# Attention of a four-layer decoder: fp32r halves replaced by fp32 operands

## The chip, the cores and the metric

One NeuronCore of a Trainium2 chip runs the whole program in one launch. The metric is the device time of an execution in microseconds (us); lower is better.

## What is computed

The reference is a decoder trunk of four layers over 256 positions and 1024 channels, all fp32. A layer is a token mixer, an output projection, a LayerNorm, a SwiGLU feed-forward of width 2816 and another LayerNorm. The mixer has 12 heads of width 64 and, beside them, 4 heads that attend to 256 memory tokens. Its kind is `i % 3`: 0 (layers 0 and 3) is attention over the keys that an indexer selects, 1 (layer 1) is dilated attention in three head groups that are merged by their softmax denominators (its values are 192 wide, four of them), 2 (layer 2) is plain causal attention at this length.

```python
for i in range(DEPTH):                       # DEPTH = 4
    kind, j = i % N_MIXERS, i // N_MIXERS
    if kind == 0:   mix = dsa_attention(q, k, v, qi, wi, ki)
    elif kind == 1: mix = dilated_attention(q, k, v)
    else:           mix = moba_attention(q, k, v)
    mo = memory_attention(qm, mk, mv)
    mixed = concat([mix, mo], -1) @ w_out[i]
    x = layer_norm(ALPHA * x + mixed, ln1_g[i], ln1_b[i])
    x = layer_norm(ALPHA * x + swiglu(x, w_gate_up[i], w_down[i]), ln2_g[i], ln2_b[i])
# attention of a head: softmax(q k^T / 8, masked) v
```

## The kernel before

All weights come once from HBM as 400 pieces of 128 x up to 1024 (`load`, line 206, on SyncE's queue, four `raw` buffers). Each piece is split in two fp32r parts: ScalarE casts the high part (`emit_hi`, L214), VectorE or GpSimd subtracts it to get the low part (`emit_lo`, L230 and L228). The activations `x` are held as two parts too. A product is then three fp32r matmuls in a row, high by high, and the two mixed ones (`mm3`, L256 to L258); a fourth, low by low, is left out.

```python
256  mm(out, lhsT=ah, rhs=bh, start=first, stop=False)
257  mm(out, lhsT=ah, rhs=bl, start=False, stop=False)
258  mm(out, lhsT=al, rhs=bh, start=False, stop=last)
```

The order on TensorE (PE) is that of the program. The main line issues the projections and the feed-forward, some 12 matmuls at a time, and after each such step `tick` advances a list of tasks, Python generators. One `yield n` of a task waits for n ticks, so that PE has other work while ScalarE (ACT) and VectorE (DVE) do the task's part. The constants `W_ROT`, `W_K`, `W_EXP`, `W_NORM`, `W_PT` are these waits. `join` ticks without issuing main work when something is needed at once. The other engines are ordered by the scheduler. Eight PSUM banks of 128 x 512 go round through all tasks (`tk(self.banks)`).

A mixer works by pairs of heads (128 columns) and by two blocks `tb` of 128 positions; block 0 sees 128 keys, block 1 sees 256. A pair's task runs so:

- `rotated` (L473): rotary positions, then two PE transposes of the fp32 rows, which put q and k with channels on partitions.
- `qk_task`: q and k are split in fp32r parts. The two parts of a head's 64 channels are laid on the two halves of the 128 partitions (`q_parts`, L267 and L272; `k_parts`, L265 and L270), and k is also copied crosswise on ACT (`k_cross`, L492 and L493). One matmul over all 128 partitions then does two products of halves at once.
- `logits` (L500 for 128 keys, L504 for 256): one or two fp32r matmuls of 256 columns a head, both heads in one bank.
- `exps` and `softmax`: mask and row minimum (L526 and, for 128 keys, L524), exponentials back into the bank (L529), then reciprocal and division of the whole matrix (L541, L542).
- `turned` (L555): PE transposes of the fp32 probabilities, one of 128 x 128 for each head and key block; the result is split in `pa`/`pb` high and low (L265, L270).
- `attend` (line 563): `mm3` of a 128-column pair of values against both heads' probabilities (256 columns), of which the two diagonal quarters are kept (`diag_out`: four instructions, L265 and L270, of 64 partitions).

The memory heads (`mem_task`) and the dilated layer (`dil_task`, `dil_combine`) use the same helpers. The indexer (`select_task`) uses `logits` with `kb` shared by its eight heads.

Of the kernel before, what the change touches and what calls it, by code (L numbers as in the profile page):

```python
# [112 lines left out]
class K:  # L113
    def __init__(self, tc, io, ctx):
# [22 lines left out]
        self.kks = one([128, 2, 2, S], "k", NKB, F32R)  # L137
        self.sts = one([128, 64], "st", 12)
        self.xT = (T([128, 8, S], F32R, "xh"), T([128, 8, S], F32R, "xl"))
        self.memT = (T([128, 8, S], F32R, "mh"), T([128, 8, S], F32R, "ml"))  # L140
        self.mk = [T([128, 2, 2, S], F32R, f"mk{i}") for i in range(2)]
        self.mv = (T([128, 2, 256], F32R, "mvh"), T([128, 2, 256], F32R, "mvl"))
# [336 lines left out]
    def q_parts(self, dst, src, scale=None):  # L479

        lo, hi = slice(0, 64), slice(64, 128)
        return [(dst[lo, 0], dst[hi, 0], src[lo], scale), (dst[hi, 1], dst[lo, 1], src[hi], scale)]

    def k_parts(self, dst, src):

        d = dst.rearrange("p h a t -> p a h t")
        n = src.shape[1]
        return d[:, 0], d[:, 1], src[:, None, :].to_broadcast([128, 2, n]), None

    def k_cross(self, dst):  # L490
        lo, hi = slice(0, 64), slice(64, 128)
        self.nc.scalar.copy(dst[hi, 0], dst[lo, 0])  # L492
        self.nc.scalar.copy(dst[lo, 1], dst[hi, 1])  # L493

    def logits(self, b, q, ks, nk):

        mm = self.nc.tensor.matmul
        for h in range(2):
            if nk == 128:
                mm(b[:, h * 256:h * 256 + 256].rearrange("p (a s) -> p a s", a=2), lhsT=q[:, h], rhs=ks[h][:, :, 0:128],  # L500
                   start=True, stop=True)
            else:
                for part in range(2):
                    mm(b[:, h * 256:h * 256 + 256], lhsT=q[:, h], rhs=ks[h][:, part], start=part == 0, stop=part == 1)  # L504

    def pair_logits(self, b, q, kb, nk):
        self.logits(b, q, [kb[:, h] for h in range(2)], nk)

    def read_logits(self, b, nk):
        if nk == 128:  # L510
            L = b.rearrange("p (h a s) -> p h a s", h=2, a=2)
            return L[:, :, 0], L[:, :, 1]
        return (b.rearrange("p (h s) -> p h s", h=2),)

    def exps(self, L, e, mn, sm, mask=None, dst=None):


        nc = self.nc
        dst = L[0] if dst is None else dst
        if mask is None:  # L520
            nc.vector.tensor_reduce(mn, L[0], op=OP.min, axis=AX.X)
        else:
            if len(L) == 2:
                nc.vector.tensor_tensor(e, L[1], mask[:, None, :].to_broadcast([128, 2, 128]), op=OP.add)  # L524
            for h in range(2):
                nc.vector.tensor_tensor_reduce(out=L[0][:, h], in0=L[0][:, h], in1=mask if len(L) == 1 else e[:, h], op0=OP.add,  # L526
                                               op1=OP.min, scale=1.0, scalar=3e38, accum_out=mn[:, h:h + 1])
        for h in range(2):
            nc.scalar.activation(dst[:, h], L[0][:, h], AF.Exp, bias=mn[:, h:h + 1], scale=-1.0, accum_out=sm[:, h:h + 1])  # L529

    def softmax(self, nk, product, mask=None):

        nc = self.nc
        b = yield from self.tk(self.banks)
        st = yield from self.tk(self.sts)
        e = yield from self.tk(self.es[nk])
        product(b)
        L = self.read_logits(b, nk)
        self.exps(L, e, st[:, 0:2], st[:, 2:4], mask)
        yield W_EXP  # L540
        nc.vector.reciprocal(st[:, 4:6], st[:, 2:4])  # L541
        nc.vector.tensor_tensor(e, L[0], st[:, 4:6, None].to_broadcast([128, 2, nk]), op=OP.mult)  # L542
        self.banks.put(b)
        self.sts.put(st)
        yield W_NORM
        return e

    def turned(self, e, nk):
# [7 lines left out]
        self.split((pT[0], pT[1], p, None))  # L556
# [5 lines left out]
    def attend(self, e, nk, vs, vi, col, mix, kb, tb):  # L562
        pT = yield from self.turned(e, nk)
        nsb = nk // 128
        while vs[vi] is None or not vs[vi][2]:
            yield 1
        v = vs[vi][0]
        b = yield from self.tk(self.banks)
        o = b[:, 0:256].rearrange("p (h t) -> p h t", h=2)
        for sb in range(nsb):  # L570
            self.mm3(o, (v[0][:, sb, col:col + 128], v[1][:, sb, col:col + 128]),
                     (pT[0][:, sb], pT[1][:, sb]), sb == 0, sb == nsb - 1)
        self.pTs[nsb].put(pT)
        self.diag_out(mix[kb], tb, o)
        self.banks.put(b)

    def diag_out(self, dst, tb, o):
        ts = slice(tb * 128, tb * 128 + 128)
        rs = [slice(h * 64, h * 64 + 64) for h in range(2)]
        self.split(*((dst[0][r, ts], dst[1][r, ts], o[r, h], None) for h, r in enumerate(rs)))  # L580

    def qk_task(self, bank, tb, kb, q, flags):
        b, p = yield from self.rotated(bank, tb)
        q[tb] = yield from self.tk(self.qs)
        k = kb[:, :, :, tb * 128:tb * 128 + 128]
        self.split(self.k_parts(k, p[:, 1]), *self.q_parts(q[tb], p[:, 0], SCALE))
        self.k_cross(k)
        self.banks.put(b)
        yield W_K
        flags.add(("k", tb))  # L590

    def head_task(self, bank, tb, kb, q, flags, masks, vs, vi, col, mix, kbi):
# [5 lines left out]
        def product(b):  # L598
            self.pair_logits(b, q[tb], kb, nk)
# [4 lines left out]
        e = yield from self.softmax(nk, product, masks[tb])  # L604
        yield from self.attend(e, nk, vs, vi, col, mix, kbi, tb)
# [7 lines left out]
    def v_piece(self, l, i, tbs, vrec):  # L613
        v = vrec[0]
        for tb in tbs:
            b = self.a_mode(self.xT, tb, ("v", l, i), tb == 1)
            self.split((v[0][:, tb], v[1][:, tb], b[:, 0:256], None))
# [7 lines left out]
    def mk_piece(self, l):  # L625
        b, p = self.t_mode(self.memT, ("mk", l, 0))
        self.split(*(self.k_parts(self.mk[pp], p[:, pp]) for pp in range(2)))
        for pp in range(2):
            self.k_cross(self.mk[pp])
# [3 lines left out]
    def mv_piece(self, l):  # L633
        for sb in range(2):
            b = self.a_mode(self.memT, sb, ("mv", l, 0), sb == 1)
            self.split((self.mv[0][:, sb], self.mv[1][:, sb], b[:, 0:256], None))
# [3 lines left out]
    def qm_piece(self, l):  # L640
        b, p = self.t_mode(self.xT, ("qm", l, 0))
        qm = [self.take(self.qms, "qm") for _ in range(2)]
        self.split(*(x for pp in range(2) for x in self.q_parts(qm[pp], p[:, pp], SCALE)))
# [4 lines left out]
    def mem_task(self, qm, pp, tb, mix):  # L648
        ts = slice(tb * 128, tb * 128 + 128)

        def product(b):
            self.pair_logits(b, qm[pp][:, :, ts], self.mk[pp], S)
        e = yield from self.softmax(S, product)
        yield from self.attend(e, S, [[self.mv, 0, True]], 0, pp * 128, mix, 6 + pp, tb)

    def mem_tasks(self, qm, mix):
        def run(pp):
# [3 lines left out]
            self.qms.put(qm[pp])  # L661
# [3 lines left out]
    def ki_task(self, bank, tb, kb, wi, kg, kbb, flags):  # L665
# [21 lines left out]
        self.split((kb[:, 0, 0, tb * 128:tb * 128 + 128], kb[:, 0, 1, tb * 128:tb * 128 + 128], b[:, 0:128], None))  # L687
# [513 lines left out]
```

## Time and profile before

| | |
|---|---|
| median of 3 runs | 1353.04 us (1347.6 to 1353.33) |
| the profiled execution | 1351.82 us, of which the span from the first to the last instruction is 1350.0 us |
| TensorE | 1287.3 us busy, 9186 matmuls, mean granted clock 0.983 |
| VectorE | 897.5 us busy, 1940 instructions |
| ScalarE | 762.9 us busy, 1512 instructions |
| GpSimd | 316.4 us busy, 277 instructions |
| DMA | 225.65 MB, 167 GB/s |

The terms below are made against the profiled execution: 1351.82 us, 1.82 us more than its span and 1.22 us under the median. A row of a group of instructions gives the line, the engine, the operation, what it writes and reads, its shape and count; then the busy time and the mean of one in ns; then the idle time of the engine just before, and who ended it. Matmuls overlap, so that their mean is longer than the step from one to the next; the step is read from the order of time. Layer 0's mixer runs from 0 to about 150 us, layer 1's from 375 to 490, layer 2's from 700 to 805, layer 3's from 1015 to 1140; the rest is output projection and feed-forward.

### The profile page before, as it was taken

What the parts mean: (1) busy time and instruction counts of PE and PEld (TensorE: products, weight loads), DVE (VectorE), ACT (ScalarE), POOL (GpSimd) and SP (SyncE); (2) the same over time, 40 slices, a digit from 0 to 9 for tenths busy, and PEclk for the clock granted to TensorE, in tenths of its full rate; (3) what the DMA queues carried; (4) which work ended last, traced back from release to release, by engine and by line L of the source; (5) the groups of instructions that cost most, each with busy time, mean ns of one, the idle gap of its engine ahead of it and who ended that gap; (6) DMA issues with size and microseconds to landing.
All of it is one profiled execution on the core that took longest, in us unless ns stands there. A gap on an engine that the chain in (4) does not pass through costs nothing. (4 is left out here: it accounts for less than half of the span.)

```text
span 1350.0 us, 24249 instructions
## 1 busy us (share of the span) xinstructions
PE 1287.3 (95%) x9186; PEld 1212.5 (90%) x9186; DVE 897.5 (66%) x1940; ACT 762.9 (57%) x1512; POOL 316.4 (23%) x277
## 2 busy tenths in 40 slices
PE   6889899999999789999999999999999899999997
PEld 5879799999999779999989989999999898899996
DVE  7887775555578886555567877555568997655555
ACT  5668754444469745444447986444445897544441
POOL 3434440000045343000034444000014533300000
PEclk9989999999999889999999999999999999999999
DMA  8443356556564136565545345666546333655551
GB/s 300 126 149 110 110 180 199 187 188 184 170 203 150 70 103 240 185 189 180 183 155 180 133 141 169 206 185 188 186 138 218 127 125 126 203 188 188 187 176 59
DMA packets 63190, 225.65 MB, mean 167 GB/s; under 512 B 7776, under 2 KB 7776, under 8 KB 63072
## 3 DMA queue, kind: packets, MB, share of 16 engines
q1 hardware_dynamic: 62784, 224.10, 50.2%
q8 instruction: 72, 1.18, 0.4%
q14 instruction: 46, 0.38, 0.1%
q10 hardware_dynamic: 288, 0.00, 0.0%
HBM read 223.02 MB, written 1.05 MB: 166 GB/s over the span
## 5 line engine op out<-in xcount | busy, mean ns | idle before, releaser
L214 ACT CAST wh<-raw 128x1024 fp32r<-128x1024 f32 (+1 forms) x402 | 420.8, 1048 | 318.6 <-PE bank L257 177.2
L230 DVE TENSOR_TENSOR wl<-raw,wh 128x1024 fp32r<-128x1024 f32 (+1 forms) x294 | 378.2, 1288 | 273.9 <-ACT wh L214 269.1
L228 POOL TENSOR_TENSOR wl<-raw,wh 128x512 fp32r<-128x512 f32 x216 | 296.7, 1399 | 727.7 <-ACT wh L214 718.2
L256 PE MATMUL bank<-xh,wh 128*128 128x256 f32 x1344 | 382.1, 284 | 0.0
L257 PE MATMUL bank<-xl,wh 128*128 128x256 f32 x1344 | 381.2, 284 | 0.0
L258 PE MATMUL bank<-xh,wl 128*128 128x256 f32 x1344 | 381.2, 284 | 0.0
L257 PEld LDWEIGHTS bank<-xl,wh 128*128 128x128 f32 x1344 | 258.6, 192 | 1.2
L256 PEld LDWEIGHTS bank<-xh,wh 128*128 128x128 f32 x1344 | 258.6, 192 | 1.3
L258 PEld LDWEIGHTS bank<-xh,wl 128*128 128x128 f32 x1344 | 258.5, 192 | 0.0
L256 PE MATMUL bank<-wh,xh 128*128 128x256 f32 (+1 forms) x768 | 228.5, 298 | 2.8 <-ACT wh L214 1.9
L257 PE MATMUL bank<-wl,xh 128*128 128x256 f32 (+1 forms) x768 | 221.6, 289 | 2.5 <-DVE wl L230 2.3
L258 PE MATMUL bank<-wh,xl 128*128 128x256 f32 (+1 forms) x768 | 221.7, 289 | 0.8 <-DVE xl L270 0.6
L256 PE MATMUL bank<-wh,fth 128*128 128x512 f32 x480 | 189.8, 395 | 0.4 <-ACT fth L265 0.4
L257 PE MATMUL bank<-wl,fth 128*128 128x512 f32 x480 | 188.2, 392 | 0.0
L258 PE MATMUL bank<-wh,ftl 128*128 128x512 f32 x480 | 188.0, 392 | 0.0
L256 PEld LDWEIGHTS bank<-wh,xh 128*128 128x128 f32 x768 | 150.1, 196 | 4.0 <-ACT wh L214 2.4
L257 PEld LDWEIGHTS bank<-wl,xh 128*128 128x128 f32 x768 | 150.1, 195 | 3.1 <-DVE wl L230 3.1
L258 PEld LDWEIGHTS bank<-wh,xl 128*128 128x128 f32 x768 | 149.9, 195 | 1.7 <-DVE xl L270 1.7
L258 PEld LDWEIGHTS bank<-wh,ftl 128*128 128x128 f32 x480 | 90.5, 189 | 19.9 <-DVE ftl L270 0.7
L256 PEld LDWEIGHTS bank<-wh,fth 128*128 128x128 f32 x480 | 90.7, 189 | 17.5 <-ACT fth L265 0.8
L257 PEld LDWEIGHTS bank<-wl,fth 128*128 128x128 f32 x480 | 90.7, 189 | 16.3
L1061 ACT CAST fth<-sil 128x256 fp32r<-128x256 f32 x80 | 32.5, 406 | 107.3 <-DVE sil L1059 107.3
(194 smaller groups left out, 1553.0 us busy)
## 6 DMA issues: line engine op xcount, KB each, us to landing
raw<-in_w SPq DMA_DIRECT2D x396, 512.0 KB, 3.9
lng<-in_ln_g SPq DMA_DIRECT2D x8, 512.0 KB, 4.0
lnb<-in_ln_b SPq DMA_DIRECT2D x8, 512.0 KB, 6.2
raw<-in_w SPq DMA_DIRECT2D x4, 492.0 KB, 4.8
x<-in_xT SPq DMA_DIRECT2D x2, 512.0 KB, 5.4
E<-in_mem SPq DMA_DIRECT2D x4, 256.0 KB, 5.6
x<-in_x SPq DMA_DIRECT2D x2, 512.0 KB, 6.0
out_x<-x SPq DMA_DIRECT2D x4, 256.0 KB, 2.2
```

What stands on the lines that cost most here:

```text
L214: self.nc.scalar.copy(c[0][:, 0:wd], self.raw[n][:, 0:wd])
L228: self.nc.gpsimd.tensor_tensor(lo[:, c], r[:, c], hi[:, c], op=OP.subtract)
L230: self.nc.vector.tensor_tensor(lo[:, 0:wd], r[:, 0:wd], hi[:, 0:wd], op=OP.subtract)
L256: mm(out, lhsT=ah, rhs=bh, start=first, stop=False)
L257: mm(out, lhsT=ah, rhs=bl, start=False, stop=False)
L258: mm(out, lhsT=al, rhs=bh, start=False, stop=last)
L1061: nc.scalar.copy(fts[i][0], s)
```

## The change

Weights, activations and the projections stay split. Inside attention nothing is split any more:

- q, k, v, the memory's keys and values, the indexer's q and k and the turned probabilities are plain fp32 tiles, each written by one copy (`self.qs`, `self.kks`, `self.vs`, `self.mk`, `self.mv`, `self.qi`, `self.pTs`). `q_parts`, `k_parts`, `k_cross`, `read_logits` and `pair_logits` go.
- `logits` is one fp32 matmul a head over that head's 64 partitions, of 128 or 256 columns, each head in a bank of its own (`tk2` takes two banks).
- `exps` writes the exponentials to SBUF and gives both banks back. The division of the matrix goes.
- `heads_out` is new: for each head and key block an fp32 matmul with the turned probabilities as stationary operand and 64 columns of v moving (192 in the dilated layer); one VectorE instruction divides by the sums; after `W_OUT` = 2 ticks a PE transpose of 128 x 128 for each 128 channels turns the output, which is then split for the output projection.
- `W_K` goes from 3 to 2, `W_NORM` goes. The buffers' numbers change as shown.

```diff
-        self.qs = one([128, 2, 128], "q", 4, F32R)
-        self.qms = one([128, 2, S], "qm", 2, F32R)
+        self.qs = one([128, 128], "q", 6)
+        self.qms = one([128, 2, S], "qm", 1)
-        self.pTs = {1: pair([128, 1, 2, 128], "pa", 2), 2: pair([128, 2, 2, 128], "pb", 2)}
-        self.vs = pair([128, 2, 256], "v", 3)
+        self.pTs = {1: one([128, 1, 2, 128], "pa", 3), 2: one([128, 2, 2, 128], "pb", 3)}
+        self.ons = one([128, 384], "on", 3)
+        v = T([128, 2, MIXW], F32, "v")
+        self.vs = Slots([v[:, :, i * 256:i * 256 + 256] for i in range(3)])
...
+    def tk2(self):
+        while len(self.banks.free) < 2:
+            yield 1
+        return [self.banks.pop(), self.banks.pop()]
+
+    def logits(self, bs, q, k, nk):
         for h in range(2):
-            if nk == 128:
-                mm(b[:, h * 256:h * 256 + 256].rearrange("p (a s) -> p a s", a=2), lhsT=q[:, h], rhs=ks[h][:, :, 0:128],
-                   start=True, stop=True)
+            r = slice(h * 64, h * 64 + 64)
+            self.nc.tensor.matmul(bs[h][:, 0:nk], lhsT=q[r], rhs=k[r, 0:nk], start=True, stop=True)
+        return [b[:, 0:nk] for b in bs]
...
         for h in range(2):
-            nc.scalar.activation(dst[:, h], L[0][:, h], AF.Exp, bias=mn[:, h:h + 1], scale=-1.0, accum_out=sm[:, h:h + 1])
+            nc.scalar.activation(e[:, h], L[h], AF.Exp, bias=mn[:, h:h + 1], scale=-1.0, accum_out=sm[:, h:h + 1])
+        for b in bs:
+            self.banks.put(b)
...
-        nc.vector.tensor_tensor(e, L[0], st[:, 4:6, None].to_broadcast([128, 2, nk]), op=OP.mult)
...
-        self.split((pT[0], pT[1], p, None))
+        self.nc.scalar.copy(pT[:, 0], p[:, 0])
+        if nsb == 2:
+            self.nc.vector.tensor_copy(pT[:, 1], p[:, 1])
...
+    def heads_out(self, pT, nsb, vs, r, outs, tb):
+        nc = self.nc
+        n = vs[0].shape[2]
+        b = yield from self.tk(self.banks)
+        for h in range(2):
+            for sb in range(nsb):
+                nc.tensor.matmul(b[:, h * n:h * n + n], lhsT=pT[:, sb, h], rhs=vs[h][:, sb], start=sb == 0, stop=sb == nsb - 1)
+        self.pTs[nsb].put(pT)
+        on = yield from self.tk(self.ons)
+        o3 = lambda t: t[:, 0:2 * n].rearrange("p (h d) -> p h d", h=2)
+        nc.vector.tensor_tensor(o3(on), o3(b), r[:, :, None].to_broadcast([128, 2, n]), op=OP.mult)
+        self.banks.put(b)
+        yield W_OUT
+        b = yield from self.tk(self.banks)
+        p = b.rearrange("p (i t) -> p i t", i=4)
+        for i in range(len(outs)):
+            nc.tensor.transpose(p[:, i], on[:, i * 128:i * 128 + 128], self.ident)
+        self.ons.put(on)
+        ts = slice(tb * 128, tb * 128 + 128)
+        self.split(*((o[0][:, ts], o[1][:, ts], p[:, i], None) for i, o in enumerate(outs)))
+        self.banks.put(b)
...
-        k = kb[:, :, :, tb * 128:tb * 128 + 128]
-        self.split(self.k_parts(k, p[:, 1]), *self.q_parts(q[tb], p[:, 0], SCALE))
-        self.k_cross(k)
+        self.nc.scalar.activation(q[tb], p[:, 0], AF.Copy, scale=SCALE)
+        self.nc.vector.tensor_copy(kb[:, tb * 128:tb * 128 + 128], p[:, 1])
...
-W_ROT, W_K, W_EXP, W_NORM, W_PT = 3, 3, 3, 2, 2
+W_ROT, W_K, W_EXP, W_PT = 3, 2, 3, 2
-W_A, W_COMB, W_KI = 2, 4, 4
+W_A, W_COMB, W_KI, W_OUT = 2, 4, 4, 2
```

How the instructions move is shown at two places of layer 2's mixer. The first is TensorE's row while the second block of a pair (`k_137` before, `k_134` after) meets its logits and the pair before it its values (`pb` are the turned probabilities, `v` the values, `E` the exponentials); "..." stands for the projections' matmuls between. Before:

```order
L500 MATMUL bank_66<-k_137,q_91 128x256 x2
...
L256 MATMUL bank_68<-pbh_106,vh_110 128x256
L257 MATMUL bank_68<-pbl_107,vh_110 128x256
L258 MATMUL bank_68<-pbh_106,vl_111 128x256
...
L555 MATMUL bank_63<-ident,E_100 128x128 x4
L504 MATMUL bank_65<-k_137,q_93 128x256 x4
```

Now:

```order
L543 MATMUL bank_66<-v,pb_107 128x64 x4
...
L491 MATMUL bank_70<-k_134,q_92 128x128
L491 MATMUL bank_64<-k_134,q_92 128x128
...
L553 MATMUL bank_63<-ident,on_110 128x128
...
L491 MATMUL bank_70<-k_134,q_93 128x256
L491 MATMUL bank_64<-k_134,q_93 128x256
```

The four logits matmuls of 256 columns of block 1 became two, in two banks; the six value matmuls of 256 columns (three for each key block, of which one key block's three are shown) became four of 64 columns, and a transpose of the divided output `on` came behind them.

The second place is ScalarE's row early in the same mixer, where q and k of the first pair (block 0, then block 1) are made and the first exponentials run. Before:

```order
L265 CAST k_136<-bank_69 128x2x128
L267 ACTIVATE q_90<-bank_69 64x128 x2
...
L492 COPY k_136<-k_136 64x2x128
L493 COPY k_136<-k_136 64x2x128
L529 ACT_TABLE_LOAD
L529 ACTIVATE bank_64,st_140<-bank_64,st_140 128x128
```

Now:

```order
L571 ACTIVATE q_90<-bank_65 128x128
...
L505 ACT_TABLE_LOAD
L505 ACTIVATE e_99,st_141<-bank_63,st_141 128x128
L505 ACTIVATE e_99,st_141<-bank_68,st_141 128x128
```

Five ScalarE instructions that made q and k of a block became one (k's copy is on VectorE), and the exponentials now go to the SBUF tile `e`.

## Rows read from the trace of the kernel before

**Rows 1.** The page, part 1 (busy time, share, instructions) and part 2, TensorE's clock.
```profile
PE 1287.3 (95%) x9186; PEld 1212.5 (90%) x9186; DVE 897.5 (66%) x1940; ACT 762.9 (57%) x1512; POOL 316.4 (23%) x277
PEclk9989999999999889999999999999999999999999
```
**Rows 2.** Windows, five mixer stretches: length, busy time per engine, clock, DMA; sum.
```profile
0.00:100.00 100.00, 76.91 (x521) 71.67 (x522) 83.91 (x263) 61.16 (x136) 40.84 (x63) 0.90 0.56 194
...
700.00:825.00 125.00, 119.91 (x897) 113.09 (x897) 98.76 (x280) 93.04 (x235) 58.37 (x46) 1.00 0.45 152
...
sum 575.00, PE 521.99 PEld 489.90 DVE 463.70 ACT 403.96 POOL 250.40; mean PE 104.40 PEld 97.98 DVE 92.74 ACT 80.79 POOL 50.08
```
**Rows 3.** Windows, layer 1's feed-forward (same columns).
```profile
525.00:700.00 175.00, 175.00 (x1225) 164.50 (x1224) 94.23 (x110) 77.76 (x103) 9.28 (x7) 1.00 0.57 182
```
**Rows 4.** Groups on TensorE by shape: logits.
```profile
L504 PE MATMUL bank<-k,q 128*128 128x256 f32 x96 | 17.9, 307 | 4.8 <-ACT E L529 2.5 <-ACT k L492 2.3
...
L500 PE MATMUL bank<-k,q 128*128 128x256 f32 x48 | 11.1, 308 | 2.2 <-ACT k L492 2.0
L504 PE MATMUL bank<-mk,qm 128*128 128x256 f32 x64 | 10.5, 286 | 0.0
...
L504 PE MATMUL bank<-k,ftl 128*128 128x256 f32 x32 | 5.7, 304 | 0.0
...
L500 PE MATMUL bank<-k,fth 128*128 128x256 f32 x16 | 3.7, 314 | 0.0
```
**Rows 5.** Groups on TensorE by shape: transposes of probabilities, and values.
```profile
L555 PE MATMUL bank<-ident,E 128*128 128x128 f32 x144 | 23.4, 287 | 5.7 <-DVE E L913 4.9 <-DVE E L542 0.8
...
L256 PE MATMUL bank<-pbh,vh 128*128 128x256 f32 x40 | 11.8, 295 | 2.8 <-ACT pbh L265 2.3 <-DVE e L542 0.2 <-DVE pbl L270 0.2
L257 PE MATMUL bank<-pbl,vh 128*128 128x256 f32 x40 | 11.7, 292 | 1.4 <-DVE pbl L270 1.4
...
L256 PE MATMUL bank<-pbh,mvh 128*128 128x256 f32 x32 | 9.6, 300 | 0.0
...
L555 PE MATMUL bank<-ident,e 128*128 128x128 f32 x40 | 8.2, 288 | 9.2 <-DVE e L913 4.8 <-DVE e L542 2.9 <-DVE q L272 0.9
...
L256 PE MATMUL bank<-pah,vh 128*128 128x256 f32 x20 | 5.9, 293 | 0.0
```
**Rows 6.** TensorE in order of time, feed-forward of layer 2: start, us, instruction.
```profile
862.11 0.39 PE L256 MATMUL bank<-wh,fth 128*128 128x512 f32 x1
...
864.83 0.39 PE L256 MATMUL bank<-wh,fth 128*128 128x512 f32 x1
...
865.62 0.28 PE L257 MATMUL bank<-xl,wh 128*128 128x256 f32 x1
...
865.98 0.28 PE L257 MATMUL bank<-xl,wh 128*128 128x256 f32 x1
```
**Rows 7.** TensorE in order of time: 128-column fp32r matmuls, layer 1's mixer.
```profile
492.35 0.27 PE L256 MATMUL bank<-pbh,vh 128*128 128x128 f32 x1
...
492.69 0.27 PE L256 MATMUL bank<-pah,vh 128*128 128x128 f32 x1
```
**Rows 8.** TensorE in order of time: four fp32 transposes, layer 2's mixer.
```profile
744.88 0.60 PE L555 MATMUL bank<-ident,E 128*128 128x128 f32 x4
745.24 0.37 PE L256 MATMUL bank<-wh,xh 128*128 128x256 f32 x1
745.44 0.28 PE L257 MATMUL bank<-wl,xh 128*128 128x256 f32 x1
```
**Rows 9.** Groups on VectorE by shape: output halves, low parts of q.
```profile
L270 DVE TENSOR_TENSOR ftl<-bank,fth 64x128 fp32r<-64x128 f32 x112 | 32.1, 287 | 25.1 <-ACT fth L265 23.0 <-PE bank L473 0.6
L272 DVE SCALAR_TENSOR_TENSOR q<-bank,q 64x128 fp32r<-64x128 f32 x96 | 27.7, 288 | 2.5
```
**Rows 10.** Groups on ScalarE by shape: one of k's two cross copies, turned probabilities.
```profile
L265 ACT CAST pbh<-bank 128x512 fp32r<-128x512 f32 x36 | 21.0, 583 | 4.2 <-PE bank L555 3.6
...
L493 ACT CAST k<-k 64x256 fp32r<-64x256 f32 x48 | 19.4, 404 | 1.0
```

More of the change, by code (lines that the diff above doesn't have):

```diff
@@ L475, in rotated @@
         return b, p
[L479 to L493, printed above, removed]
@@ L538, in softmax @@
-        L = self.read_logits(b, nk)
-        self.exps(L, e, st[:, 0:2], st[:, 2:4], mask)
+        bs = yield from self.tk2()
+        self.exps(bs, product(bs), e, st[:, 0:2], st[:, 2:4], mask)
         yield W_EXP
-        nc.vector.reciprocal(st[:, 4:6], st[:, 2:4])
-        nc.vector.tensor_tensor(e, L[0], st[:, 4:6, None].to_broadcast([128, 2, nk]), op=OP.mult)
[L543 to L546, printed above, removed]
+        self.nc.vector.reciprocal(st[:, 4:6], st[:, 2:4])
@@ L548, in turned @@
+        return e, st
     def turned(self, e, nk):
@@ L567, in attend @@
         v = vs[vi][0]
[L568 to L580, printed above, removed]
+        yield from self.heads_out(pT, nk // 128, [v[:, :, col + h * 64:col + h * 64 + 64] for h in range(2)], st[:, 4:6],
+                                  [mix[kb]], tb)
+        self.sts.put(st)
     def qk_task(self, bank, tb, kb, q, flags):
@@ L596, in head_task, with product @@
         nk = 128 * (tb + 1)
-        def product(b):
-            self.pair_logits(b, q[tb], kb, nk)
+        def product(bs):
+            L = self.logits(bs, q[tb], kb, nk)
             self.qs.put(q[tb])
@@ L603, in product @@
                 self.kks.put(kb)
-        e = yield from self.softmax(nk, product, masks[tb])
-        yield from self.attend(e, nk, vs, vi, col, mix, kbi, tb)
+            return L
+        e, st = yield from self.softmax(nk, product, masks[tb])
+        yield from self.attend(e, st, nk, vs, vi, col, mix, kbi, tb)
         v = vs[vi]
@@ L626, in mk_piece @@
         b, p = self.t_mode(self.memT, ("mk", l, 0))
-        self.split(*(self.k_parts(self.mk[pp], p[:, pp]) for pp in range(2)))
-        for pp in range(2):
-            self.k_cross(self.mk[pp])
+        self.nc.scalar.copy(self.mk, p)
         self.banks.put(b)
@@ L641, in qm_piece @@
         b, p = self.t_mode(self.xT, ("qm", l, 0))
-        qm = [self.take(self.qms, "qm") for _ in range(2)]
-        self.split(*(x for pp in range(2) for x in self.q_parts(qm[pp], p[:, pp], SCALE)))
+        qm = self.take(self.qms, "qm")
+        self.nc.scalar.activation(qm, p, AF.Copy, scale=SCALE)
         self.banks.put(b)
@@ L649, in mem_task @@
         ts = slice(tb * 128, tb * 128 + 128)
[L651 to L654, printed above, removed]
+        e, st = yield from self.softmax(S, lambda bs: self.logits(bs, qm[:, pp, ts], self.mk[:, pp], S))
+        yield from self.attend(e, st, S, [[self.mv, 0, True]], 0, pp * 128, mix, 6 + pp, tb)
     def mem_tasks(self, qm, mix):
+        left = [0, 1]
         def run(pp):
@@ L660, in run @@
                 yield from self.mem_task(qm, pp, tb, mix)
-            self.qms.put(qm[pp])
+            left.remove(pp)
+            if not left:
+                self.qms.put(qm)
         return [self.spawn(run(pp)) for pp in range(2)]
@@ L693, in qi_task @@
         b, p = yield from self.rotated(bank, tb)
+        t = self.qi[tb][c]
+        self.nc.scalar.copy(t, p)
         for i in range(2):
-            qi[tb, 2 * c + i] = mix[2 + 2 * c + i][tb].rearrange("p (h t) -> p h t", h=2)
-        self.split(*(x for i in range(2) for x in self.q_parts(qi[tb, 2 * c + i], p[:, i])))
+            qi[tb, 2 * c + i] = t[:, i]
         self.banks.put(b)
@@ L710, in select_task @@
                 yield 1
-            b = yield from self.tk(self.banks)
-            rl = yield from self.tk(self.es[nk])
-            self.logits(b, qi[tb, pr], [kb[:, 0]] * 2, nk)
-            L = self.read_logits(b, nk)
-            r = L[0]
-            if len(L) == 2:
-                nc.scalar.copy(rl, L[1])
-                nc.vector.tensor_tensor(r, r, rl, op=OP.add)
-            nc.scalar.activation(r, r, AF.Relu)
+            bs = yield from self.tk2()
+            L = self.logits(bs, qi[tb, pr], kb, nk)
+            for r in L:
+                nc.scalar.activation(r, r, AF.Relu)
             if pr == 3:
@@ L873, in dil_task @@
         st = parts[jp, tb, "st"]
-        b = yield from self.tk(self.banks)
         e = yield from self.tk(self.es[nk])
-        self.pair_logits(b, q[tb], kb, nk)
+        bs = yield from self.tk2()
+        L = self.logits(bs, q[tb], kb, nk)
         self.qs.put(q[tb])
```

103 lines of the change are left out of this document (36 added, 67 removed).

## The prediction, made before the changed kernel had run

> **What bounds the kernel now.** I read the page's busy shares first, then windows by stage, then the groups on TensorE with the idle time before them, and last TensorE's order of time for the step from one matmul to the next. TensorE is busy for 1287.3 of 1350.0 us; VectorE and ScalarE for 897.5 and 762.9 [rows 1]. The average hides two kinds of stage. In a feed-forward TensorE is busy without a gap, 175.00 of 175.00 us, with VectorE at 94 and ScalarE at 78 [rows 3]: nothing that the change touches lies there. In the five mixer stretches TensorE is busy for 521.99 of 575.00 us, so 53.0 us of idle lie there, and 23.1 of them in the first 100 us, where VectorE is the busiest engine at 83.91 and the granted clock is 0.90 instead of 1.00 [rows 2]. In layer 2's mixer TensorE has 119.91 of 125.00, VectorE 98.76, ScalarE 93.04 [rows 2]. So TensorE bounds the mixers too, except in the first 100 us, but there it also waits for the other two. Idle directly before attention's own matmuls is 4.8 + 2.2 us at the logits [rows 4] and 5.7 + 2.8 + 1.4 + 9.2 us at transposes and values [rows 5], 26.1 us together. These are the places where fewer split instructions can help.
>
> The step between matmuls is what each costs when TensorE is the bound. 512 columns of fp32r take (864.83 - 862.11)/12 = 0.227 us, 256 columns (865.98 - 865.62)/3 = 0.120 [rows 6]; the difference is 0.418 ns a column, and about 0.012 us is fixed. 128 columns don't take half of 0.120, but (492.69 - 492.35)/3 = 0.113 [rows 7]: there the load of 128 weight columns sets the step. Four fp32 transposes cost (745.44 - 744.88 - 0.12)/4 = 0.110 each [rows 8], the first matmul behind them being late. I use 0.12 for 256 columns and 0.11 for 128 and for a transpose.
>
> **What leaves TensorE.** Logits: 96 + 48 + 64 + 32 + 16 = 256 matmuls of 256 columns [rows 4], 256 x 0.12 = 30.7 us. Values: 40 + 32 + 20 = 92 groups of three with 256 columns [rows 5], 276 x 0.12 = 33.1, and the dilated layer's 12 groups with 128 columns, 36 x 0.11 = 4.0. Together 67.8 us.
>
> **What comes to TensorE.** Of the logits each head and block has one fp32 matmul of 64 rows: 48 + 16 = 64 with 128 columns, and half of 96 + 64 + 32, which is 96, with 256 columns [rows 4]. Of the values each head and key block has one. Over 52 tasks outside the dilated layer (18 with one key block, 34 with two) that is 18 x 2 + 34 x 4 = 172 of 64 columns; the dilated layer has 12 of 192. Then 52 + 12 = 64 transposes turn the output. The transposes before the values stay.
>
> No row shows an fp32 matmul that multiplies, so its price needs bounds. Below: it could cost no more than the rows with one pass, 0.11 up to 192 columns and 0.12 at 256. Then 64 x 0.11 + 96 x 0.12 + 172 x 0.11 + 12 x 0.11 + 64 x 0.11 = 45.8 us come. Above: two operands split in halves make four products, of which the kernel issues three by hand; four fp32r matmuls, each with its own weight load, are 0.48 at 256 columns and 0.44 below. Then 64 x 0.44 + 96 x 0.48 + 184 x 0.44 + 7.0 = 162.2 us come. The nearest row by work is the kernel's own group of three, 0.36 at 256 columns, nearer to the upper end. I take four products that stream 0.418 ns a column each but share a load for each half of the stationary operand, so two loads of 0.11 and two fixed parts of 0.012. That is 0.45 at 256 columns, 0.24 at 128, 0.345 at 192, and at 64, where loads rule, 0.22. So 64 x 0.24 + 96 x 0.45 = 58.6 for logits, 172 x 0.22 + 12 x 0.345 = 42.0 for values, 7.0 for transposes: 107.6 us come, 39.8 us more than leave. By the bounds it is -22.0 to +94.4.
>
> The Trainium skill, "FP8 and Floating Point Precision", TensorE Precision Notes, says that true FP32 takes four passes through the array (high by high, the two mixed ones, low by low). No row here shows it; four passes at the bare stream would be 0.43 us at 256 columns, so by it the sum would be close to mine, and it speaks against the change.
>
> **What leaves the other engines.** VectorE loses 112 half outputs (32.1 us) and 96 low parts of q (27.7) [rows 9] and gets 48 copies of k and 64 low parts of the output, at 287 ns [rows 9] 32.1 us: -27.7. The divisions only shrink from a matrix to an output, the low parts of K, V and the probabilities go and are left out of this sum, which is a floor. ScalarE loses both cross copies of k, 2 x 19.4, and half of the 21.0 us at the turned probabilities [rows 10], some 49 us, before the smaller ones. Neither engine bounds a mixer after layer 0's head, so this is worth only the waits that it ends. I credit 20 of the 26.1 us of idle before attention's matmuls, because the logits lose the cross copy that releases them and the values lose the low part, while one wait of each kind stays (mask and minimum, exponential, copy). I credit 5 us more in the first 100 us, where VectorE is the bound. Bounds of this credit: nothing, if the new copies and the division at the output are waited for in the same way, and all 53.0 us. The new wait is at the output's transpose: it stands behind a division of 128 columns with two ticks of projections (about 24 matmuls, 2.9 us) between, and TensorE's queue behind it is the next projection. Two ticks cover it unless VectorE is more than 2 us behind. With the logits in two banks, eight banks serve fewer tasks at once, but they return before the division instead of after it: nothing.
>
> The DMA's bytes, the casts of weights (L214, L230, L228) and their queue are unchanged; a longer mixer only gives them time. **The sum:** 1351.8 + 39.8 - 25 = 1366.6 us against the profiled execution, 1.22 us under the median shown. I say 1366.
>
> **The rivals.** *Slower by far: a weight load for each product.* The upper price above, 1351.8 + 94.4 - 25 = 1421. For it: 128-column fp32r matmuls already step by their load [rows 7]; against it, one load can serve two streams.
>
> *Faster: the two heads run beside each other.* The two logits matmuls of a pair stand next to each other in the order, use different halves of the rows and different banks. If the halves work at once, the logits cost half, 58.6/2 = 29.3 less: 1337. It decides as soon as two such matmuls step by less than half of one. For it: nothing in their data ties them; against it: every matmul in this trace covers all 128 rows, so no row shows it. The Trainium skill, "TensorEngine Tiling (Array Packing)", Key Properties, says that row tiles can load and multiply in parallel; by that rule the result is this rival's, and no run here shows it yet.
>
> *Slower: changing between halves and the whole array empties the pipe, and waits stay.* A 256-column matmul lasts 0.284 us by its record but steps by 0.12 [rows 6], so 0.16 us of it is covered by the next one. If that cover is lost when a pair begins and when it ends, 80 pairs x 2 x 0.16 = 26 us are added: 1392. The same page says under Key Properties that a change of the tiling mode drains TensorE; by that the time is this rival's, and no row shows it. The same figure results without a drain if the whole credit of 25 us fails.
>
> *No change.* The idle that ends is not 25 but about 40 us of the 53.0, and the time stays at 1352. For it: ScalarE falls most where it is fullest; against it: 27 of the 53 us stand before work that attention does not touch.
>
> **How the numbers follow.** Chances: forecast 0.45, with a range of its own from 1348 to 1385 (credit 10 to 45); load for each product 0.13; heads beside each other 0.20; drain or no credit 0.14; no change 0.08. A measurement of this kernel can tell about 0.5%, 6.8 us, from no change. Faster by more than that: the side-by-side case nearly whole and a little of the forecast's low end, 0.22. Within it: no change, a fifth of the forecast and a little of the rest, 0.18. Slower: 0.60. The range goes from 1333 to 1410: it takes in forecast, no change, drain and most of the side-by-side case, and leaves out the load for each product and the rest, about 0.2. Most of the chance lies on the slower side because the product's own work on the bounding engine rises by more than the idle that it can end.
>
> **What would show it.** In the changed profile the 64-column value matmuls should step by about 0.22 us and the 256-column logits by about 0.45; 0.44 and 0.48 would show the load for each product, 0.11 and 0.12 the lower bound. Two logits of a pair that step by less than 0.24 would show the heads beside each other; a first projection behind a pair that starts more than 0.1 us late would show the drain. VectorE's busy time should fall by at least 28 us and ScalarE's by at least 30. Idle of TensorE in the mixer stretches should fall from 53.0 to about 30. The prediction is wrong if TensorE's busy time does not rise, or if idle falls by more than 40 us.

## The result, and the profile after

The changed kernel takes 1341.81 us (1339.27 to 1344.45), the kernel before 1353.18 beside it: a ratio of 0.9916 with a 95% interval of 0.9895 to 0.9937. It is 11 us faster, where 13 us slower was forecast. The profiled execution of the changed kernel, 1339.27 us, is the fastest of its four. The page of the changed kernel, parts 1 and 2, has beside [rows 1]:

```profile
PE 1305.3 (98%) x9370; PEld 1205.4 (90%) x9370; DVE 776.9 (58%) x1660; ACT 651.3 (49%) x1216; POOL 313.3 (23%) x277
...
PEclk9999999999999999999999999999999999999999
```

TensorE's busy time rose by 18 us, VectorE's fell by 121, ScalarE's by 112, and the low digits of the clock are gone. The mixers by windows, cut at the same projection matmul in both kernels; first the kernel before (more exact cuts than [rows 2], same columns):

```profile
0.00:100.70 100.70, 77.61 (x527) 72.36 (x528) 83.91 (x263) 61.58 (x137) 40.84 (x63) 0.90 0.55 193
100.70:175.10 74.40, 69.63 (x492) 64.70 (x491) 53.22 (x171) 56.67 (x156) 31.65 (x24) 0.98 0.34 114
375.10:500.20 125.10, 111.95 (x803) 105.79 (x802) 99.62 (x278) 82.40 (x216) 53.05 (x40) 0.93 0.41 139
700.10:825.10 125.00, 119.91 (x897) 113.09 (x896) 98.76 (x280) 93.14 (x235) 58.37 (x46) 1.00 0.46 152
1000.10:1152.10 152.00, 144.18 (x1041) 134.94 (x1039) 130.50 (x411) 111.93 (x280) 68.49 (x57) 1.00 0.41 138
sum 577.20, PE 523.28 PEld 490.88 DVE 466.00 ACT 405.72 POOL 252.40; mean PE 104.66 PEld 98.18 DVE 93.20 ACT 81.14 POOL 50.48
```

The changed kernel:

```profile
0.00:91.10 91.10, 78.66 (x555) 68.34 (x556) 65.97 (x218) 48.68 (x104) 40.21 (x63) 0.96 0.61 211
91.10:162.70 71.60, 71.60 (x526) 63.84 (x525) 33.27 (x132) 38.81 (x108) 30.31 (x24) 1.00 0.36 121
362.70:477.60 114.90, 110.16 (x808) 98.88 (x807) 78.06 (x230) 60.92 (x157) 52.28 (x40) 1.00 0.45 152
677.50:803.80 126.30, 125.75 (x951) 114.57 (x950) 69.56 (x219) 69.10 (x167) 57.51 (x45) 1.00 0.45 148
978.80:1139.20 160.40, 155.05 (x1102) 138.25 (x1100) 99.70 (x328) 84.33 (x205) 68.08 (x58) 0.99 0.39 131
sum 564.30, PE 541.22 PEld 483.89 DVE 346.57 ACT 301.86 POOL 248.40; mean PE 108.24 PEld 96.78 DVE 69.31 ACT 60.37 POOL 49.68
```

Layer 0 became 12.4 us shorter and layer 1 10.2; layer 2 became 1.3 us longer and layer 3 8.4. TensorE's idle in the mixers fell from 53.9 to 23.1 us. The granted clock, the share of full speed that TensorE was allowed, was 0.90, 0.98 and 0.93 in the first three stretches before. That is 10.1 + 1.5 + 8.8 = 20.4 us short of a full clock, in part while TensorE stood idle; after the change 5.2 us are left.

TensorE's groups, for [rows 4, 5]:

```profile
L526 PE MATMUL bank<-ident,E 128*128 128x128 f32 x144 | 22.0, 274 | 1.2 <-DVE E L894 1.0
...
L543 PE MATMUL bank<-v,pb 128*128 128x64 f32 x144 | 18.1, 269 | 0.0
...
L491 PE MATMUL bank<-k,q 64*128 64x256 f32 x96 | 17.2, 435 | 2.0 <-DVE k L572 2.0
...
L491 PE MATMUL bank<-k,qi 64*128 64x128 f32 x32 | 5.0, 366 | 3.7 <-DVE bank L462 3.7
```

The idle before logits is 6.2 us (2.0, 3.7 and 0.5 at a smaller group) instead of 7.0, that before the transposes 1.2 instead of 14.9, that before the values none instead of 4.2. Together that is 7.4 us where it was 26.1. An fp32 matmul leaves two records: 48 with `k,q` of 256 columns are counted 96 times. Their steps stand in the order of time of layer 2's mixer:

```profile
752.36 0.28 PE L262 MATMUL bank<-wh,xl 128*128 128x256 f32 x1
752.57 0.70 PE L491 MATMUL bank<-k,q 64*128 64x256 f32 x4
753.20 0.39 PE L260 MATMUL bank<-wh,xh 128*128 128x256 f32 x1
753.43 0.28 PE L261 MATMUL bank<-wl,xh 128*128 128x256 f32 x1
...
754.85 1.00 PE L543 MATMUL bank<-v,pb 128*128 128x64 f32 x8
755.69 0.39 PE L526 MATMUL bank<-ident,e 128*128 128x128 f32 x2
```

A pair with 128 keys stands in layer 1's mixer:

```profile
384.11 0.28 PE L262 MATMUL bank<-xh,wl 128*128 128x256 f32 x1
384.32 0.49 PE L491 MATMUL bank<-k,q 64*128 64x128 f32 x4
384.74 0.39 PE L260 MATMUL bank<-xh,wh 128*128 128x256 f32 x1
384.96 0.28 PE L261 MATMUL bank<-xl,wh 128*128 128x256 f32 x1
```

A pair of heads with 256 keys costs (753.43 - 0.12) - (752.36 + 0.12) = 0.83 us, a pair with 128 keys by the same reading 0.61. In front of a transpose instead of a projection it is 0.78 and 0.57. Eight value records take (755.69 - 754.85)/8 = 0.105 each, so an fp32 matmul of 64 columns takes 0.21.

With these steps TensorE's own work can be summed in every run: each matmul's count by its step (0.12, 0.227 and 0.15 for 256, 512 and 328 columns, 0.11 for 128 and for a transpose, 0.11 and 0.162 a record of the values, and the two prices of a pair). What is left of a stretch is lost to waits, to the low clock and to late matmuls. The table gives a mixer's length and in brackets what is lost of it, us, cut at the same projection matmuls; the feed-forwards of layers 0 to 2 lose under 0.5 us in every run and are left out, and so is the end of the program, which loses 9 to 12. The prices are rounded and every pair is taken at 0.83 or 0.61, so a sum is good to 1 or 2 us, and some losses come out below nothing. The rows are profiled executions, which lie up to 4 us beside the median of their kernel.

```
                     layer 0 head  layer 0 rest  layer 1        layer 2       layer 3       whole span: work, lost
before               100.7 (33.1)  74.4 ( 8.3)   125.1 (21.7)   125.0 ( 8.4)  152.0 (10.9)  1257.4, 92.6
after                 91.1 (17.6)  71.6 (-1.1)   114.9 ( 5.6)   126.3 ( 0.1)  160.4 ( 6.9)  1297.9, 39.6
values alone          98.5 (29.3)  69.6 ( 1.1)   112.8 ( 9.2)   122.1 ( 1.6)  151.8 ( 6.8)  1269.4, 58.7
logits alone          92.2 (20.2)  70.2 (-0.1)   113.9 ( 4.8)   122.8 ( 0.5)  158.9 ( 9.3)  1285.9, 46.7
before, values twice 102.0 (32.9)  78.1 ( 4.1)   124.1 (11.7)   129.8 ( 3.9)  160.8 (10.3)  1294.5, 73.8
after, values twice   95.6 (19.4)  80.6 (-1.0)   120.3 ( 3.5)   137.9 ( 0.1)  173.0 ( 7.9)  1339.9, 40.4
after, VectorE load   94.8 (21.3)  72.7 ( 0.0)   124.9 (15.6)   128.7 ( 2.4)  165.4 (11.9)  1297.9, 63.1
before, no q low      95.8 (28.1)  71.4 ( 5.3)   119.0 (15.6)   122.8 ( 6.2)  149.7 ( 8.6)  1257.4, 73.6
before, no k cross   100.3 (32.7)  69.6 ( 3.5)   119.0 (15.6)   121.4 ( 4.8)  152.1 (11.0)  1257.4, 77.9
fp32 logits 0 and 1   87.5 (14.0)  72.1 (-0.7)   116.7 ( 7.4)   121.8 ( 1.3)  151.4 ( 6.4)  1283.6, 40.8
fp32 logits 2 and 3   97.7 (28.5)  69.5 ( 1.0)   113.9 (10.3)   126.5 ( 0.3)  162.6 ( 9.0)  1283.6, 61.0
```

Work rose by 40.5 us and losses fell by 53.0: that is the result. Losses fell in every mixer, by 15.5 and 9.4 us in layer 0, 16.1 in layer 1, 8.3 in layer 2 and 4.0 in layer 3. Layers 2 and 3 became longer because the added work there is more than that.

### The profile page after: what moved, and what is told of

Same layout as the page of the kernel before. It is cut to its first block, busy times and chain, and to the rows that moved or that the text cites. A ratio compares the mean times of both kernels' runs of the same rounds, so it can differ in the third digit from the quotient of the medians.

```text
span 1337.5 us, 23972 instructions
## 1 busy us (share of the span) xinstructions
PE 1305.3 (98%) x9370; PEld 1205.4 (90%) x9370; DVE 776.9 (58%) x1660; ACT 651.3 (49%) x1216; POOL 313.3 (23%) x277
## 4 chain that ended last, share of the span: by engine, by line
PE 89%; DVE 5%; issue 2%; POOL 2%; DMA 1%; ACT 1%; SPq 0%; DVEq 0%; POOLq 0%; ACTq 0%
PE bank L260 27%; PE bank L262 26%; PE bank L261 26%; PE bank L491 3%; PE bank L543 3%; POOL wl L232 2%; PE bank L526 2%; DMA raw<-in_w 1%; PE bank L477 1%; DVE wl L234 1%; PE bank L326 1%; DVE E L894 1%; PE bank L553 1%; ACT wh L218 0%; DVE e L894 0%
## 5 line engine op out<-in xcount | busy, mean ns | idle before, releaser
L232 POOL TENSOR_TENSOR wl<-raw,wh 128x512 fp32r<-128x512 f32 x216 | 293.7, 1383 | 726.5 <-ACT wh L218 690.8
L260 PE MATMUL bank<-wh,xh 128*128 128x256 f32 (+1 forms) x768 | 231.4, 301 | 1.3 <-ACT xh L269 0.9
L260 PEld LDWEIGHTS bank<-wh,fth 128*128 128x128 f32 x480 | 90.3, 188 | 18.8 <-issue 1.3
```

The source lines that it names most:

```text
L232: self.nc.gpsimd.tensor_tensor(lo[:, c], r[:, c], hi[:, c], op=OP.subtract)
```

## The experiments

**Each half alone.** Values, division and output as after, logits as before; then the reverse. In both the exponentials go to SBUF and give their banks back before the division, as in the changed kernel.

```diff
-        self.exps(bs, product(bs), e, st[:, 0:2], st[:, 2:4], mask)   # after
+        product(b)                                    # split q and k, pair_logits
+        self.exps(self.read_logits(b, nk), e, st[:, 0:2], st[:, 2:4], mask)
```

> The second half of the change alone: logits stay in fp32r halves as before, values, division and output are as after. TensorE's own work rises by about 12 us (values 37.0 to 42.1, output transposes 7.0). Theory 'relief' (the gain is work that leaves VectorE and ScalarE, so that TensorE waits less; TensorE's added work is paid in full): about half of the relief comes here, 1335 to 1345 us. Rival 'ride' (the added TensorE work costs nothing because it fills idle time, and the relief is small): 1348 to 1356.

1329.75 us, ratio 0.9831 (0.9817 to 0.9846): better than either kernel.

```diff
-        product(b)                                    # before
+        bs = yield from self.tk2()
+        self.exps(bs, product(bs), e, st[:, 0:2], st[:, 2:4], mask)   # plain q and k
         nc.vector.reciprocal(st[:, 4:6], st[:, 2:4])
-        nc.vector.tensor_tensor(e, L[0], ...
+        nc.vector.tensor_tensor(e, e, ...
```

> The first half alone: fp32 logits over 64 rows a head, with the matrix divided, turned and split as before. TensorE's own work rises by about 28 us (logits 30.7 to 59). 'Relief': half of the relief against 28 us, 1350 to 1362 us. 'Ride': 1340 to 1350, since nothing is paid and some waits go.

1336.02 us, 0.9876 (0.9861 to 0.9891). Both lie below the range that "relief" gave them, and the second below that of "ride" too. Alone they save 23.5 and 17 us, together 11. By the table they end 33.9 and 45.9 us of losses, together only 53.0, while the work that they add, 12.0 and 28.5, is added in full. A part of what they end is the same. Both halves give the banks back early, and no run has that step alone, so what it is worth is open.

**The ticks.**

```diff
-W_ROT, W_K, W_EXP, W_PT = 3, 2, 3, 2
+W_ROT, W_K, W_EXP, W_PT = 3, 3, 5, 2
```

> The changed kernel with the ticks of before: W_K 3 instead of 2, and 5 ticks between exponentials and transposes instead of 3 (before had 3 and 2). 'Relief': 1340 to 1346, no change. Rival 'ticks' (the gain is the shorter chain of waits that the program order prescribes): 1350 or more.

1337.39 us, 0.9883 (0.9867 to 0.9900), some 4 us under the changed kernel with the new ticks, with intervals that just overlap. "Ticks" falls.

**TensorE's work alone, doubled in both kernels.**

```diff
-        for sb in range(nsb):                     # before; both places that call mm3 on values
+        for sb in [*range(nsb)] * 2:
```

> The kernel before with every value product issued twice (the second overwrites the first with the same sums): 312 more fp32r matmuls, 37 us of TensorE work at the measured steps, nothing else. 'Relief' (added TensorE work is paid): 1378 to 1392 us. 'Ride' (it fills the idle 53 us of the mixers): under 1365.

```diff
-        for h in range(2):                        # after, heads_out
+        for h in [0, 1, 0, 1]:
```

> The changed kernel with every value product issued twice: 184 more fp32 matmuls, 42 us of TensorE work. 'Relief': TensorE bounds the changed kernel nearly everywhere, so all is paid, 1378 to 1388 us. 'Ride': less than 20 us more, under 1362.

Before: 1370.14 us, 1.0130 (1.0115 to 1.0145). 37 us of work cost 16.9; the work's sum rose by 37.1, the losses fell by 18.8, half of them in layer 1. After: 1379.45, 1.0193 (1.0168 to 1.0218): 42 us of work cost 37.6, and the losses stay at 40. Both theories had a part. In the kernel before, half of this added TensorE work fills time that was lost anyway; in the changed kernel TensorE is nearly full and pays.

**Load put back on one engine, its results unused.** For ScalarE:

```diff
+        for _ in range(3):                        # qk_task, behind q and k
+            self.nc.scalar.copy(self.scr[0][:, 0:128], kb[:, tb * 128:tb * 128 + 128])
+            self.nc.scalar.copy(self.scr[0][:, 0:128], q[tb])
...
+        self.nc.scalar.copy(self.scr[0][:, 0:256], pT[:, 0]...)      # turned
```

> The changed kernel with copies to a scratch tile that nobody reads put back on ScalarE: six of 128 columns behind each of the 48 blocks of q and k, one of 256 behind each of the 56 turned probabilities, some 100 us of ScalarE time in the mixers; no chain gets a step longer. 'Relief by load' (ScalarE's and VectorE's queues were too full): 10 us or more are given back, 1352 or more. Rival 'relief by steps' (each chain had fewer steps, the load itself was no matter): 1340 to 1347.

For VectorE the same places, with two and three subtractions.

> The same on VectorE: two subtractions of 128 columns behind each block of q and k, three of 256 behind each turned matrix, some 98 us of VectorE time in the mixers, results unused. 'Relief by load': 10 us or more are given back, 1352 or more, and more than on ScalarE, because VectorE is the fullest engine in layer 0. 'Relief by steps': 1340 to 1347.

ScalarE, whose busy time rose by 82 us to 733.2: 1341.90 us, no change. VectorE, by 126.5 us:

```profile
PE 1315.4 (97%) x9370; PEld 1213.0 (89%) x9370; DVE 903.4 (66%) x1924; ACT 649.9 (48%) x1216; POOL 319.2 (23%) x277
```

1358.56 us, 1.0039 (1.0025 to 1.0052) of the kernel before, 16.8 more than the changed kernel. In the profiled executions its losses rose by 23.5, of which 10.0 in layer 1; but that execution, 1362.76 us, is the slowest of its ten, and the medians' 16.8 is the better size. So VectorE's load, back at the level of the kernel before (897.5), matters. ScalarE's, beside the path, does not show, though less of it was put back: 82 us of the 112 that had gone.

**The whole array for each head.** q is padded with zeros to 128 rows.

```diff
-            r = slice(h * 64, h * 64 + 64)
-            self.nc.tensor.matmul(bs[h][:, 0:nk], lhsT=q[r], rhs=k[r, 0:nk], start=True, stop=True)
+            self.nc.tensor.matmul(bs[h][:, 0:nk], lhsT=q[:, h], rhs=k[:, 0:nk], start=True, stop=True)
```

> The changed kernel with q padded by zeros to 128 rows a head, so that each logits matmul covers the whole array and two heads cannot run beside each other; one more small ScalarE copy a block. Theory: what side-by-side running saves, the change between half and whole array costs again (a pair of 256 columns takes 0.83 us in the changed kernel, two whole-array products would be about 0.90), so the time stays within 5 us of 1342. Rival 'side by side pays': 15 us more or worse.

1339.79 us, 0.9903 (0.9875 to 0.9931), the same. A pair now has its four records in a row, here with 256 keys in layer 2's mixer and with 128 keys in layer 1's:

```profile
729.24 0.27 PE L554 MATMUL bank<-ident,on 128*128 128x128 f32 x1
729.35 1.03 PE L492 MATMUL bank<-mk,qm 128*128 128x256 f32 x4
730.03 0.47 PE L262 MATMUL bank<-wh,xh 128*128 128x256 f32 x1
730.33 0.28 PE L263 MATMUL bank<-wl,xh 128*128 128x256 f32 x1
...
383.25 0.28 PE L264 MATMUL bank<-xh,wl 128*128 128x256 f32 x1
383.37 0.61 PE L492 MATMUL bank<-k,q 128*128 128x128 f32 x4
383.74 0.36 PE L262 MATMUL bank<-xh,wh 128*128 128x256 f32 x1
383.94 0.28 PE L263 MATMUL bank<-xl,wh 128*128 128x256 f32 x1
```

With 256 keys a pair costs (730.33 - 0.12) - 729.35 = 0.86 us, against 0.83. With 128 keys it costs (383.94 - 0.12) - (383.25 + 0.12) = 0.45, against 0.61: there the two halves of the array are the dearer way.

**One step taken from the kernel before.** First q's low parts, which stay zero (the logits see q's high part alone):

```diff
-        self.split(self.k_parts(k, p[:, 1]), *self.q_parts(q[tb], p[:, 0], SCALE))
+        self.split(self.k_parts(k, p[:, 1]))
+        self.q_high(q[tb], p[:, 0], SCALE)        # ScalarE alone; the memory heads likewise
```

> The kernel before without the low parts of q (heads and memory heads; they stay zero, so logits see q's high part only): 112 VectorE instructions and 34.5 us of VectorE time go, each from the path between q and its logits; TensorE's work is the same. 'Relief on VectorE' (98 us of extra VectorE time cost the changed kernel 17 us): 6 us or more faster, 1347 or less. Rival (VectorE's load does not matter in the kernel before, only in a kernel that is fuller on TensorE): within 4 us of 1353.

1333.58 us, 0.9858 (0.9843 to 0.9872). Then k's cross copies, which put each part of k on the other half of the partitions (the memory's likewise):

```diff
-        self.k_cross(k)
```

> The kernel before without k's cross copies (logits then use a wrong half of k): 112 ScalarE instructions and 48.6 us of ScalarE time go, and the step between k and its logits that L504 and L500 waited for. TensorE's and VectorE's work are the same. 'Relief by steps' or by ScalarE: 6 us or more faster, 1347 or less. 'VectorE alone': 1349 to 1354.

1334.86 us, 0.9865 (0.9849 to 0.9882). Neither changes TensorE's work; 37 us less on VectorE end 19.0 us of losses, 47 us less on ScalarE, on k's path, end 14.7 (18 by the medians). "VectorE alone" falls for the kernel before: there ScalarE counts too. Each removal takes load from an engine and a step from the path to the logits, and these two runs don't separate them.

**More distance, more steps.** Values alone with `W_EXP` 5:

> The version with fp32 values alone, and 5 ticks instead of 3 between exponentials and transposes: if the longer distance hides what TensorE still waits for there (58.7 us of its span are not work), some us faster than 1329.75; if the tasks then end too late for the output projection, slower.

1335.05 us, 5.3 slower than with 3. A copy through a scratch tile on k's path in the changed kernel:

```diff
-        self.nc.vector.tensor_copy(kb[:, tb * 128:tb * 128 + 128], p[:, 1])
+        self.nc.vector.tensor_copy(t[:, 0], p[:, 1])
+        self.nc.scalar.copy(t[:, 1], t[:, 0])
+        self.nc.scalar.copy(kb[:, tb * 128:tb * 128 + 128], t[:, 1])
```

> The changed kernel with two more steps in a row on k's path: VectorE copies it to a scratch tile, ScalarE copies it there and then into its place (96 ScalarE copies of 128 columns, VectorE's work the same). 100 us of ScalarE load beside the path cost nothing, so a longer time is the steps: 'relief by steps' 1348 or more; otherwise 1337 to 1345.

1343.63 us, 0.9931 (0.9911 to 0.9950), not to be told from the changed kernel. In the changed kernel two more steps on k's path are covered; whether they would be in the kernel before, with its fuller VectorE, this run does not show.

**fp32 logits by layer.** Values in fp32 throughout; q, k and the memory's keys are allocated for each layer in the type that it uses.

```diff
+F32_LAYERS = (0, 1)                       # the mirror: (2, 3)
+        self.f32 = l in F32_LAYERS        # mixer; chooses plain or split q and k
```

> Values in fp32 in all layers, logits in fp32 in layers 0 and 1 alone, in halves in layers 2 and 3. By stages of the runs so far: where TensorE still waits (layers 0 and 1) fp32 logits end more waiting than they add work, where it is full (2 and 3) they are paid. 'Local to the stage': the sum of the better stages, 1318 to 1326 us. Rival 'the relief is shared over the program' (one queue's backlog carries over, stages don't add): 1329 or more.

> The mirror: logits in fp32 in layers 2 and 3, in halves in layers 0 and 1. 'Local to the stage': the sum of the worse stages, 1338 to 1350 us. Rival: 1330 to 1336, like the versions with one half of the change.

1325.54 us, 0.9799 (0.9778 to 0.9821), and 1343.50 us, 0.9928 (0.9903 to 0.9953). Both lie where stages that don't touch each other put them. In layer 3 logits in halves leave 151.4 us and fp32 ones take 162.6; in layer 0's head it is 97.7 with halves and 87.5 without. In layer 1 the fp32 logits don't pay once the values are fp32: 116.7 us against 112.8 with values alone, and 114.9 against 113.9 between the changed kernel and the mirror. With fp32 values the table puts the gain of fp32 logits in layer 0's head; a version with them in layer 0 alone was not run. The version with fp32 logits in layers 0 and 1 beats both kernels, by 27.5 and 16.3 us. Its page, part 1:

```profile
PE 1294.4 (98%) x9338; PEld 1210.0 (91%) x9338; DVE 806.4 (61%) x1746; ACT 693.3 (52%) x1340; POOL 315.0 (24%) x277
```

## Why the prediction was wrong

**TensorE's work was right.** 39.8 us more were forecast, 40.5 are found by the table: logits about 59 for 58.6, values about 42 for 42.0, output transposes 7.0 for 7.0. The price at 64 columns was 0.22 and is 0.21 to 0.22, so the load for each product (1421 us) did not come. For the four passes that the Trainium skill states in "FP8 and Floating Point Precision", TensorE Precision Notes, the trace agrees in time: half of 0.86 is 0.43 us a head at 256 columns, as the rule gave.

**The logits' total was right by two errors.** I priced two heads one after the other. They do run beside each other: the four records of a pair last 0.435 us on average, 1.74 together, and stand within 0.70 us. But the whole pair takes 0.83, because each record lasts longer than alone (four alone step by 0.86/4 = 0.215), the pair starts 0.09 us late and the projection behind it another 0.11 late (0.23 instead of 0.12 to the next one). The lateness in front belongs to the change between halves and the whole array: the whole-array pair starts on time (729.35 - 729.24 = 0.11, a transpose's step). The lateness behind does not show that. There the whole-array pair has 0.30 instead of 0.12, without any change of halves, so the sign that I named for the drain could not single it out. Of the two rules that the Trainium skill gives in "TensorEngine Tiling (Array Packing)", Key Properties, the trace agrees with tiles that work in parallel. It agrees with a drain at a change of the mode in front of a pair, where 80 pairs at 0.09 us are 7 us and not the rival's 26.

That the rival with heads beside each other said 1337, near the result, is luck: its pairs were to cost half, and they cost 0.83 us.

**The step that failed is the credit for ended waits: 25 us, bounds nothing to 53.0.** The losses fell by 53.0 us, twice the credit. (That this equals the upper bound, the idle of the mixers, is chance.) With 53.0 in place of 25 the sum is 1351.8 + 40.5 - 53.0 = 1339.3, the time of the profiled execution. The 53.0 us have three parts. TensorE's idle in the whole span fell by 30.5 us (from 62.7 to 32.2). Time lost to the low clock while TensorE was busy fell by 12.1, as shown below. Some 10 are left, matmuls that started late and the error of the sums.

The credit was right where I looked: of the 26.1 us before attention's own matmuls 18.7 went, and I had credited 20. Elsewhere idle fell by 11.8 us, and I had credited 5. For the clock and the late starts, some 22 us, I had credited nothing.

So the first misreading is that I read losses as idle only. In the kernel before, in layer 0's head, TensorE waits 2.04 us for the cross copy and then runs at half the clock, in steps of 0.21 us instead of 0.12:

```profile
68.93 1.01 PE L500 MATMUL bank<-k,q 128*128 128x256 f32 x2 [2.04 <-ACT k L492]
69.74 0.42 PE L256 MATMUL bank<-wh,xh 128*128 128x256 f32 x1
69.95 0.41 PE L257 MATMUL bank<-wl,xh 128*128 128x256 f32 x1
70.17 0.41 PE L258 MATMUL bank<-wh,xl 128*128 128x256 f32 x1
70.38 0.42 PE L256 MATMUL bank<-wh,xh 128*128 128x256 f32 x1
```

These count as busy. Apart from the last microseconds of the program the trace before has nine stretches at a granted clock of 0.5, each in or behind waits of 0.7 to 6.2 us; the trace after has three. Windows over them, before (this stretch and the sum of the nine) and after (the sum of the three):

```profile
68.90:72.30 3.40, 3.37 (x14) 3.14 (x14) 3.32 (x17) 1.21 (x3) 1.77 (x3) 0.50 0.32 88
...
sum 40.90, PE 34.38 PEld 33.24 DVE 35.89 ACT 16.76 POOL 13.19; mean PE 3.82 PEld 3.69 DVE 3.99 ACT 1.86 POOL 1.47
...
sum 10.20, PE 10.20 PEld 8.69 DVE 6.86 ACT 3.65 POOL 2.70; mean PE 3.40 PEld 2.90 DVE 2.29 ACT 1.22 POOL 0.90
```

TensorE was busy for 34.38 us in them at half the clock, which loses 17.2; after the change 10.20 us lose 5.1. The whole span lost 92.6 us where idle is 62.7. The clock's digits were in [rows 1] and its 0.90 in [rows 2]; the work's sum by steps would have shown the rest before the change ran.

Second, I credited idle almost only in front of attention's own matmuls and held that VectorE and ScalarE bound no mixer after layer 0's head. But the change also ended waits in front of work that it leaves as it was. Before the transposes of q and k and of the indexer's key TensorE's idle fell from 12.9 to 4.0 us, first before, then after:

```profile
L473 PE MATMUL bank<-ident,nat 128*128 128x128 f32 x112 | 22.1, 280 | 12.9 <-DVE kd L681 7.0 <-DVE nat L460 5.9
...
L477 PE MATMUL bank<-ident,nat 128*128 128x128 f32 x112 | 23.6, 293 | 4.0 <-DVE st L462 3.3 <-DVE kd L667 0.8
```

VectorE releases these transposes, and it had less in its queue. The two removals from the kernel before show that 37 or 47 us less on either engine already end 19.0 and 14.7 us of losses. They also warn against reading a single wait as its price: without the cross copies layer 0's head, where the wait above stands, still loses 32.7 of its 33.1 us; what they end lies behind it.

What ended the 53.0 us is told in parts that were measured apart. Added TensorE work fills lost time: 18.8 of 37 us. VectorE's load: 126 us put back cost 16.8 by the medians. Two extra steps on k's path cost 1.8 and ScalarE's load beside the path 0.1, both within what the medians can tell. How these overlap, and so the exact share of each, was not separated. The shorter chain from the exponentials to the values and the early return of the banks were not tried alone. So that the change ends waits, and how many, is measured; which of its steps ends most of them stays open.

**The rivals.** "No change" had the direction right, a credit larger than 25, and was given 0.08. It looked for about 40 us in idle alone, where 30.5 went. The remark against it, that 27 of the 53 us stand before work that attention does not touch, was wrong: a good third of the idle that ended stood there. Of the signs named, VectorE's and ScalarE's fall came (121 and 112 us); the idle of the mixers fell to 23.1 where 30 was given. The signs of being wrong did not come: TensorE's busy time rose by 18.0 us and the mixers' idle fell by 30.8, less than 40. Both look at busy and idle alone, and so they missed the clock as the credit did.

## What to carry to other kernels

Before crediting waits, sum the bounding engine's work from counts and steps of its dense stretches and take it from the span: what is left holds idle, half-rate clock and late starts together, and was 92.6 us here where idle was 62.7. Price added work by stage: in the kernel with losses half of it was free, in the full one it was paid, so one part of a change may be right for some layers and wrong for others (1325.54 us against 1341.81). When two changes end the same waits, their gains don't add, but their costs do.

## What the runs showed of the hardware that was not expected

Two 64-row fp32 matmuls on the two halves of the array run beside each other, and yet gain next to nothing over whole-array ones: 0.83 against 0.86 us a pair at 256 columns, and 0.61 against 0.45 at 128, where they lose. An fp32 matmul is two records. With 64 columns each steps by 0.105 to 0.11 us, the same as 128 columns of fp32r [rows 7] and of whole-array fp32 (0.45/4), so fewer than 128 columns save nothing. That the load of the stationary operand, 128 columns in all three, is the reason fits but was not tried. 82 us more of ScalarE work beside the path cost nothing measurable, 126 us more of VectorE work 16.8 us.
